# Top-k searches of a hidden expert selection placed behind each head's scores; exponential and step lengths of the open selections moved

## The chip, the core and the metric

The kernel runs on one core of a Trainium2 chip. The metric is the device time of one execution in microseconds (us). Engines are named as in the profile: PE (TensorE, matrix products; PEld its weight loads), DVE (VectorE), ACT (ScalarE), POOL (GpSimd), SP (SyncE, which issues the DMAs).

## The reference, cut

Two layers of a backbone: layer 0 mixes by short convolution and grouped-query attention, layer 1 by a bidirectional recurrence (RWKV-7). After each mixer stands the PEER feed-forward network, and the change is in how its experts are selected.

```
def peer_ffn(xn, w_q, sub_keys, u_tab, v_tab):      # T tokens in chunks of 128
        q = (xc @ w_q).reshape(n, 8, 2, 128)                        # 8 heads, two halves
        s = einsum('nhpd,hpkd->nhpk', q, sub_keys)                  # scores against 2 x 128 keys
        s1, i1 = top_k(s[:, :, 0], 16);  s2, i2 = top_k(s[:, :, 1], 16)
        cand_s = s1[..., :, None] + s2[..., None, :]                # 256 candidates of a head
        cand_i = i1[..., :, None] * 128 + i2[..., None, :]
        top_s, pos = top_k(cand_s, 16);  idx = take_along_axis(cand_i, pos)
        gate = softmax(top_s)
        act = gelu(einsum('nd,nhkd->nhk', xc, u_tab[idx]))
        return einsum('nhk,nhkd->nd', gate * act, v_tab[idx])
```

There are 128 x 128 = 16384 experts of width 1024, 256 latent and 256 context tokens. Layer 0 runs the network for both streams, layer 1 for the latent stream alone.

## The kernel before, in words

**Dense experts.** The kernel doesn't gather rows of the tables. It runs through all 16384 experts in 128 blocks E of 128, for 256 tokens at once (a pass); layer 0 has two passes, E = 0 to 255, layer 1 one. For each E: `prep_u` splits a block of the first table into a high part (uh, on ACT) and a low part (ul, half on DVE and half on POOL); `first` makes 24 products on PE (L1249 to L1251) and ACT's gelu (L1121); `gate` multiplies by the gate matrix G on DVE (L1128), splits the product into gwh (ACT) and gwl (DVE, both through `split`, L1244 and L1245); `second` makes 12 products with the second table (L1143), whose split `prep_v` leaves vl to POOL. G holds for each token the softmax weight of each expert, and is made by `gen` = `spread` (one-hots on DVE: oh L1029, eq L1033, two A L1035) and `gather` (32 products on PE, L1045, and a copy on ACT, L1046), 16 steps for 32 blocks of experts. A has one buffer.

**Selection.** The class `TopK` has three parts, all mainly on DVE. `keys` finds the 16 best of 128 scores, 4 columns a head (two halves, two blocks of 128 tokens), five instructions each (L83 to L87). `pair` takes two heads: candidates (L107), their best 16 (L117 to L121), the differences tm to the best (L125), the exponential of tm on ACT (L126), then the indices by comparisons and sums (L132 to L165, the helper `pick` among them), and the normalised weights (L170 to L175). It yields three times between these parts. `finish` transposes the results on PE.

**Open selection.** `Peer.start` runs twice, ahead of the first pass of layer 0 (about 300 to 506 us) and ahead of the pass of layer 1 (about 2900 to 3101 us). Tasks are written by generators: `score` and `keys` of eight heads, `ahead` (32 first products, W0 to W31, which need no selection), and `finish` (transposes, casts to i16 and g16, then 16 steps `gen`). `weave` takes the task with the lowest clock next and adds the number that it yields, so these numbers set the order in which the instructions are written; a list scheduler then places them on the engines.

**Hidden selection.** The selection of layer 0's second pass is done during its first: `select_shadow` is a generator that `beside` steps through in four slots of each E, from E = 32 to 92, such that NSEL = 162.4 units are spread evenly over them (2.7 for one E). A yield without a number is 1.0; WKEYS and WPAIR are 2.2. It makes the norm of the second chunk, then for each head two strips of the score weights (wh, wl), the products, and the score tile sc, which it stores to DRAM (sD). When all eight heads' scores are there, it opens the pool sht, loads the scores back (scl) and runs `keys` and `pair` over all heads one behind the other.

## Time and profile before

| | |
|---|---|
| median of 3 runs | 3780.04 us (3778.81 to 3786.54) |
| the profiled execution, its own time | 3783.13 us |
| its span in the profile | 3781.4 us |
| mean granted clock of PE | 0.943 |
| PE busy | 3411.8 us (90%) |
| DVE busy | 2511.7 us (66%) |
| ACT busy | 1728.7 us (46%) |
| POOL busy | 1754.1 us (46%) |

Busy time is the sum of an engine's instructions; the shares are means over stages with different limits, so they don't say which engine sets the pace in one stage. The profiled execution is one run of the program: its times are compared with each other, and its own time, not the median, is what a sum of its rows starts from. An idle time in brackets behind a row, or a wait, names what ended it.

### The profile page before, as it was taken

What the parts mean: (1) busy time and instruction counts of PE and PEld (TensorE: products, weight loads), DVE (VectorE), ACT (ScalarE), POOL (GpSimd) and SP (SyncE); (2) the same over time, 40 slices, a digit from 0 to 9 for tenths busy, and PEclk for the clock granted to TensorE, in tenths of its full rate; (3) what the DMA queues carried; (4) which work ended last, traced back from release to release, by engine and by line L of the source; (5) the groups of instructions that cost most, each with busy time, mean ns of one, the idle gap of its engine ahead of it and who ended that gap; (6) DMA issues with size and microseconds to landing.
All of it is one profiled execution on the core that took longest, in us unless ns stands there. A gap on an engine that the chain in (4) does not pass through costs nothing.

```text
span 3781.4 us, 74053 instructions
## 1 busy us (share of the span) xinstructions
PE 3411.8 (90%) x29543; PEld 2980.4 (79%) x29543; DVE 2511.7 (66%) x5230; ACT 1728.7 (46%) x2813; POOL 1754.1 (46%) x984
## 2 busy tenths in 40 slices
PE   7998789999889989999999999887787788999999
PEld 5678777998778778987788788786676776888898
DVE  3569887558964447546777655376878889666522
ACT  4343445554444445555444444453223345555544
POOL 1121644655455545444333333433434543666676
PEclk9999899999999999999999999987698889999999
DMA  7364655876588977775555565551024334555554
GB/s 237 122 217 151 218 174 194 265 249 226 191 293 287 323 256 240 248 236 191 193 180 191 182 218 192 189 167 37 21 68 139 112 102 150 179 179 179 178 186 155
DMA packets 337538, 710.57 MB, mean 188 GB/s; under 512 B 41220, under 2 KB 199560, under 8 KB 336168
## 3 DMA queue, kind: packets, MB, share of 16 engines
q1 hardware_dynamic: 337192, 705.84, 56.0%
q8 instruction: 231, 3.78, 0.4%
q14 instruction: 115, 0.94, 0.1%
HBM read 624.45 MB, written 81.30 MB: 187 GB/s over the span
## 4 chain that ended last, share of the span: by engine, by line
PE 56%; DVE 23%; issue 5%; POOL 3%; DMA 2%; ACT 2%; SPq 0%; DVEq 0%; POOLq 0%; ACTq 0%
PE acc L1143 19%; PE mm L1249 9%; PE mm L1250 9%; PE mm L1251 9%; DVE A L1035 3%; DVE mm L1128 2%; DVE oh L1029 2%; DVE prod L465 1%; PE mm L1045 1%; DVE TT L468 1%; DVE eq L1033 1%; PE mm L840 1%; PE mm L730 1%; DVE wl L1245 1%; DVE gwl L1245 1%
## 5 line engine op out<-in xcount | busy, mean ns | idle before, releaser
L1245 POOL TENSOR_TENSOR vl<-raw,vh 128x1024 fp32r<-128x1024 f32 x352 | 877.9, 2494 | 857.3 <-ACT vh L1244 773.8
L1249 PE MATMUL mm<-xh,uh 128*128 128x256 f32 x3072 | 909.6, 296 | 38.5 <-ACT uh L1097 35.1
L1250 PE MATMUL mm<-xh,ul 128*128 128x256 f32 x3072 | 898.0, 292 | 35.5 <-DVE ul L1102 22.9
L1251 PE MATMUL mm<-xl,uh 128*128 128x256 f32 x3072 | 889.2, 289 | 0.0
L1102 POOL TENSOR_TENSOR ul<-raw,uh 128x512 fp32r<-128x512 f32 x320 | 498.8, 1568 | 485.1 <-ACT uh L1097 441.5
L1249 PEld LDWEIGHTS mm<-xh,uh 128*128 128x128 f32 x3072 | 608.3, 198 | 57.3 <-ACT uh L1097 37.7
L1250 PEld LDWEIGHTS mm<-xh,ul 128*128 128x128 f32 x3072 | 610.1, 199 | 50.3 <-DVE ul L1102 27.2
L1251 PEld LDWEIGHTS mm<-xl,uh 128*128 128x128 f32 x3072 | 610.1, 199 | 16.1 <-issue 16.1
L1143 PE MATMUL acc<-vh,gwh 128*128 128x512 f32 x1536 | 499.9, 406 | 12.3 <-ACT gwh L1244 9.3
L1244 ACT CAST vh<-raw 128x1024 fp32r<-128x1024 f32 x384 | 403.1, 1050 | 232.4 <-issue 124.4
L1143 PE MATMUL acc<-vh,gwl 128*128 128x512 f32 x1536 | 484.4, 396 | 5.3 <-DVE gwl L1245 4.3
L1143 PE MATMUL acc<-vl,gwh 128*128 128x512 f32 x1536 | 482.9, 396 | 5.5 <-POOL vl L1245 5.4
L1128 DVE TENSOR_TENSOR mm<-mm,G 128x256 f32<-128x256 f32 x320 | 136.5, 427 | 470.3 <-ACT mm L1121 469.7
L1035 DVE TENSOR_TENSOR A<-eq,g 128x512 f16<-128x512 f16 x384 | 330.2, 886 | 115.5 <-PE mm L1045 64.7
L1097 ACT CAST uh<-raw 128x1024 fp32r<-128x1024 f32 x384 | 399.8, 1042 | 8.3 <-DMA raw<-in_peer_u_dram 8.1
L1121 ACT ACTIVATE mm<-mm 128x256 f32<-128x256 f32 x320 | 119.3, 373 | 512.4 <-PE mm L1251 509.0
L1143 PEld LDWEIGHTS acc<-vh,gwl 128*128 128x128 f32 x1536 | 289.0, 189 | 79.5 <-DVE gwl L1245 12.7
L1143 PEld LDWEIGHTS acc<-vl,gwh 128*128 128x128 f32 x1536 | 289.6, 190 | 74.7 <-POOL vl L1245 10.1
L1143 PEld LDWEIGHTS acc<-vh,gwh 128*128 128x128 f32 x1536 | 262.8, 191 | 57.9 <-ACT gwh L1244 12.0
L1029 DVE TENSOR_TENSOR oh<-iotaR,i 128x2048 f16<-128x2048 f16 x192 | 257.5, 1341 | 19.0 <-ACT i L939 16.7
L1244 ACT CAST gwh<-mm 128x256 fp32r<-128x256 f32 x384 | 142.9, 375 | 266.3 <-DVE mm L1128 263.4
L1102 DVE TENSOR_TENSOR ul<-raw,uh 128x512 fp32r<-128x512 f32 x192 | 187.1, 974 | 86.0 <-ACT uh L1097 85.9
(418 smaller groups left out, 5969.2 us busy)
## 6 DMA issues: line engine op xcount, KB each, us to landing
raw<-in_peer_u_dram SPq DMA_DIRECT2D x384, 512.0 KB
raw<-in_peer_v_dram SPq DMA_DIRECT2D x384, 512.0 KB
low<-ul SPq DMA_DIRECT2D x128, 512.0 KB
ul<-low SPq DMA_DIRECT2D x128, 512.0 KB
wraw<-in_ada_w_dram SPq DMA_DIRECT2D x48, 1024.0 KB
wraw<-in_peer_wq_dram SPq DMA_DIRECT2D x16, 1024.0 KB
wraw<-in_ev_w_in_dram SPq DMA_DIRECT2D x9, 1024.0 KB
wraw<-in_ev_w_out_dram SPq DMA_DIRECT2D x8, 1024.0 KB
```

Of the source, the lines that this page charges most:

```text
L1029: V.tensor_tensor(oh, self.iotaR[:, None].to_broadcast([128, 8, 128, 2]), per_token(i16[:, 1]).to_broadcast([128, 8, 128, 2]), ALU.is_equal)
L1035: V.tensor_tensor(A[:, i], eq, per_token(g16[:, i]).to_broadcast(sh), ALU.mult)
L1097: k.S.copy(uh, ur)
L1102: (le or (k.V, k.P)[i]).tensor_sub(ul[:, t], ur[:, t], uh[:, t].bitcast(F32))
L1121: self.k.S.activation(W, H, AF.Gelu)
L1128: self.k.V.tensor_mul(W2, W, self.GT[E // 32][:, E % 32])
L1143: self.k.T.matmul(self.ACC[n][2 * tb + dh], lhsT=a[:, 128 * tb:128 * tb + 128], rhs=b[:, 512 * dh:512 * dh + 512], start=e == 0 and a is w ...
L1244: self.last_copy = self.S.copy(hi, src).ins
L1245: (le or self.V).tensor_sub(lo, src, hi.bitcast(F32))
L1249: self.T.matmul(out, lhsT=ah, rhs=bh, start=start, stop=False)
L1250: self.T.matmul(out, lhsT=al, rhs=bh, start=False, stop=False)
L1251: self.T.matmul(out, lhsT=ah, rhs=bl, start=False, stop=stop)
```

## The change

Three edits. In `pair`, the exponential of tm is emitted behind the comparison g2 of its last part instead of in its first part. In `Peer.start`, a step of `keys` yields 2.9 instead of 1.1, and a step of `gen` 3.2 instead of 2.0. In `select_shadow`, the keys of a head follow directly behind its scores, and a pair directly behind its second head; scores are read from the tile sc, with no store to DRAM and no load back (16 of each fall away); the keys are loaded by heads, 128x256 eight times instead of 128x512 four times; and the pool sht is opened together with shw. The number of units of the hidden selection and its start and end stay.

```diff
@@ -123,7 +123,6 @@
         tm = tile([4, 16], F32, "tm")
         T4 = T16.rearrange("p b h k -> p (b h) k")
         V.tensor_tensor(tm, T4, T4[:, :, 0:1].to_broadcast([128, 4, 16]), ALU.subtract)
-        k.S.activation(tm, tm, AF.Exp)
         yield
 
         XF = tile([2, 16, 4], F16, "XF")
@@ -165,6 +164,7 @@
         V.tensor_sub(bb, PF, bb)
         g2 = tile([16, 16, 4], F16, "ge")
         V.tensor_tensor(g2, over_a(bb), over_k(k.io16), ALU.is_equal)
+        k.S.activation(tm, tm, AF.Exp)
         pick(g2, XF[:, 1], sel[:, 1])
         z = tile([2, 4], F32, "z")
         V.tensor_reduce(z[:, 0], tm, axis=AX.X, op=ALU.add)
@@ -906,7 +906,7 @@
         def keys(hd):
             for a in range(2):
                 tk.keys(hd, a, sc[hd][:, a])
-                yield 1.1
+                yield 2.9
             if hd % 2:
                 for _ in tk.pair(hd // 2):
                     yield 4.0
@@ -945,7 +945,7 @@
             yield 2.0
             for j in range(16):
                 self.gen(0, j)
-                yield 2.0
+                yield 3.2
 
         tasks = {}
         for hd in range(8):
@@ -1719,8 +1719,6 @@
     def select_shadow(self, layer, st, hd, xD, iD):
 
         I, tc, S, T, Y = self.I, self.tc, self.S, self.T, self.Y
-        sD = [self.dp.tile([128, 16, 128], F32, name=f"sD{i}") for i in range(2)]
-        kD = self.dp.tile([128, 16, 128], F32, name="kD")
         with tc.tile_pool(name="shx", bufs=1, reuse_waits="tile") as px:
             xs = [px.tile([128, 8, 256], F32R, name=f"xs{i}") for i in range(2)]
             with tc.tile_pool(name="shn", bufs=1, reuse_waits="tile") as pn:
@@ -1734,14 +1732,15 @@
                     self.split(xs[0][:, k], xs[1][:, k], xT[:, k], self.P)
                     yield
                 Y.dma_start(xD, xT)
-            with tc.tile_pool(name="shw", bufs=1, reuse_waits="tile") as pw:
+            with tc.tile_pool(name="sht", bufs=1, reuse_waits="tile") as pool, tc.tile_pool(name="shw", bufs=1, reuse_waits="tile") as pw:
+                tk = TopK(self, pool, f"{layer}s")
                 ws = self.strips(pw, self.score_specs(layer, 128), ahead=0, n=128, nr=1, nh=1)
                 for q in range(4):
-                    kT = pw.tile([128, 4, 128], F32, name="keysT")
-                    Y.dma_start(kT, I["peer_keys"][layer][:, 4 * q:4 * q + 4])
-                    yield
                     for hh in range(2):
                         hd_ = 2 * q + hh
+                        kT = pw.tile([128, 2, 128], F32, name="keysT")
+                        Y.dma_start(kT, I["peer_keys"][layer][:, 2 * hd_:2 * hd_ + 2])
+                        yield 0.5
                         qs = pw.tile([128, 2, 256], F32, name="qs")
                         for c in range(2):
                             wh, wl = next(ws)
@@ -1757,32 +1756,25 @@
                         pv = p.rearrange("p (a c k) -> p a c k", a=2, c=2)
                         for a in range(2):
                             for c in range(2):
-                                T.matmul(pv[:, a, c], lhsT=qs[:, c, 128 * a:128 * a + 128], rhs=kT[:, 2 * hh + c], start=True, stop=True)
+                                T.matmul(pv[:, a, c], lhsT=qs[:, c, 128 * a:128 * a + 128], rhs=kT[:, c], start=True, stop=True)
                         yield
                         sc = pw.tile([128, 2, 2, 128], F32, name="sc")
                         S.copy(sc, pv)
-                        for a in range(2):
-                            Y.dma_start(sD[a][:, 2 * hd_:2 * hd_ + 2], sc[:, a])
                         yield
-        with tc.tile_pool(name="sht", bufs=1, reuse_waits="tile") as pool:
-            tk = TopK(self, pool, f"{layer}s")
-            for hd_ in range(8):
-                for b in range(2):
-                    sc = pool.tile([128, 2, 128], F32, name="scl", bufs=3)
-                    Y.dma_start(sc, sD[b][:, 2 * hd_:2 * hd_ + 2])
-                    tk.keys(hd_, b, sc)
-                    yield WKEYS
-                if hd_ % 2:
-                    for _ in tk.pair(hd_ // 2):
+                        for b in range(2):
+                            tk.keys(hd_, b, sc[:, b])
+                            yield WKEYS
+                    for _ in tk.pair(q):
                         yield WPAIR
                     yield WPAIR
-            def put(b, p):
-                iT = pool.tile([128, 3, 128], F32, name="iT", bufs=2)
-                S.copy(iT, p)
-                Y.dma_start(iD[:, :, 128 * b:128 * b + 128], iT)
-
-            tk.finish(put, self.mm)
-            yield
+
+                def put(b, p):
+                    iT = pool.tile([128, 3, 128], F32, name="iT", bufs=2)
+                    S.copy(iT, p)
+                    Y.dma_start(iD[:, :, 128 * b:128 * b + 128], iT)
+
+                tk.finish(put, self.mm)
+                yield
 
 
     def rwkv_cols(self):
```

Where this moves instructions, in the order in which each engine has them:

In the hidden selection, DVE before the change. gate mm, ul and gwl are the ordinary work of an expert, A, oh and eq the one-hots; the first search is the row L83, and all others follow from there on:

```order
L1128 TENSOR_TENSOR mm_9970<-mm_9970,G_6823 128x256
L1102 TENSOR_TENSOR ul_10083<-raw_9960,uh_10081 128x512
L1245 TENSOR_TENSOR gwl_10078<-mm_9970,gwh_10077 128x256
L1035 TENSOR_TENSOR A_10179<-eq_10180,g16_4206 128x512 x2
L1029 TENSOR_TENSOR oh_10362<-iotaR_3276,i16_4205 128x2048
L1033 TENSOR_TENSOR eq_10365<-iotaR_3276,i16_4205 128x512
L1128 TENSOR_TENSOR mm_10088<-mm_10088,G_6823 128x256
L1102 TENSOR_TENSOR ul_10172<-raw_10086,uh_10170 128x512
L1245 TENSOR_TENSOR gwl_10167<-mm_10088,gwh_10166 128x256
L83 MAX M_10148<-scl_10151 128x8 x2
L84 MAX_INDEX X_10149<-M_10148,scl_10151 128x8
```

DVE after the change, at its first search. wl is the low part of score weights, which before stood ahead of every search:

```order
L1245 TENSOR_TENSOR gwl_7928<-mm_7815,gwh_7927 128x256
L1245 TENSOR_TENSOR wl_8552<-wraw_7832,wh_8551 128x1024
L1035 TENSOR_TENSOR A_8006<-eq_8007,g16_4566 128x512 x2
L1029 TENSOR_TENSOR oh_8200<-iotaR_3216,i16_4565 128x2048
L1033 TENSOR_TENSOR eq_8203<-iotaR_3216,i16_4565 128x512
L1128 TENSOR_TENSOR mm_7938<-mm_7938,G_5415 128x256
L1102 TENSOR_TENSOR ul_7999<-raw_7936,uh_7997 128x512
L83 MAX M_7129<-sc_7990 128x8
L1245 TENSOR_TENSOR gwl_7994<-mm_7938,gwh_7993 128x256
L84 MAX_INDEX X_7130<-M_7129,sc_7990 128x8
L85 MATCH_REPLACE s2_8024<-M_7129,sc_7990 128x128
L83 MAX M_7129<-sc_7990 128x8
```

The first search now follows on its head's scores, with the weights of later heads still to come; it is the first of eight such bursts of keys, every second with a pair behind it, and between them lie the scores of the next head.

In the open selection of layer 1, ACT before the change, at its fourth exponential (tm; W is the gelu of a first product, uh the cast for one):

```order
L1121 ACTIVATE W8_34638<-mm_34613 128x256
L1097 CAST uh_34697<-raw_34640 128x1024
L126 ACT_TABLE_LOAD
L126 ACTIVATE tm_34922<-tm_34922 128x64
L1121 ACT_TABLE_LOAD
L1121 ACTIVATE W9_34693<-mm_34668 128x256
L1097 CAST uh_34767<-raw_34695 128x1024
```

ACT after the change, at the same place:

```order
L1121 ACTIVATE W8_34511<-mm_34486 128x256
L1097 CAST uh_34573<-raw_34513 128x1024
L167 ACT_TABLE_LOAD
L167 ACTIVATE tm_35185<-tm_35185 128x64
L1121 ACT_TABLE_LOAD
L1121 ACTIVATE W9_34557<-mm_34532 128x256
L1097 CAST uh_34622<-raw_34559 128x1024
```

The exponential stands between the same W8 and W9 (its line number is that of the instruction ahead of its new place); the other seven of the open selections stay between their gelus in the same way.

Further on in the same stage, ACT before the change, where the indices (i16, g16) are cast and the copies G of the gathers begin:

```order
L1097 CAST uh_35114<-raw_35041 128x1024
L1121 ACTIVATE W17_35094<-mm_35069 128x256
L939 CAST i16_35098<-acc_35100 128x2x128
L940 ACTIVATE g16_35099<-acc_35100 128x128
L939 CAST i16_35098<-acc_35107 128x2x128
L940 ACTIVATE g16_35099<-acc_35107 128x128
L1097 CAST uh_35190<-raw_35096 128x1024
L1121 ACTIVATE W18_35144<-mm_35119 128x256
L1097 CAST uh_35306<-raw_35146 128x1024
L1046 COPY G_35148<-acc_35156 128x16x32
L1121 ACTIVATE W19_35220<-mm_35195 128x256
```

ACT after the change, at the same casts:

```order
L1121 ACTIVATE W27_35391<-mm_35366 128x256
L939 CAST i16_35395<-acc_35397 128x2x128
L940 ACTIVATE g16_35396<-acc_35397 128x128
L939 CAST i16_35395<-acc_35404 128x2x128
L940 ACTIVATE g16_35396<-acc_35404 128x128
L1097 CAST uh_35487<-raw_35393 128x1024
L1121 ACTIVATE W28_35483<-mm_35458 128x256
L1097 CAST uh_35562<-raw_35485 128x1024
L1046 COPY G_35411<-acc_35419 128x16x32
L1121 ACTIVATE W29_35517<-mm_35492 128x256
L1097 CAST uh_35637<-raw_35519 128x1024
L1046 COPY G_35411<-acc_35528 128x16x32
```

The casts moved from behind W17 to behind W27. Before, copies G and gelus alternate from there to W31; after, four copies stand among the last four gelus, and twelve follow with no gelu between them, behind two casts vh and two casts uh for the first experts of the loop. In layer 0 the casts stay where they were, and five gathers instead of about one for each gelu stand ahead of W31, eleven behind it.

## Rows read from the trace of the kernel before

**Rows 1.** The page's chain that ended last, by engine.

```profile
PE 56%; DVE 23%; issue 5%; POOL 3%; DMA 2%; ACT 2%; SPq 0%; DVEq 0%; POOLq 0%; ACTq 0%
```

**Rows 2.** Windows: length, busy PE, PEld, DVE, ACT, POOL, PE clock, DMA share, GB/s.

```profile
694.50:881.00 186.50, 186.50 (x1593) 172.04 (x1592) 99.33 (x125) 95.55 (x139) 112.81 (x54) 1.00 0.75 245
881.00:898.80 17.80, 17.80 (x142) 16.08 (x140) 16.24 (x76) 8.94 (x14) 11.40 (x6) 1.00 0.85 293
898.80:1087.00 188.20, 163.63 (x1266) 144.24 (x1264) 184.16 (x612) 85.37 (x123) 94.40 (x49) 0.94 0.61 207
```

**Rows 3.** Timeline of ACT (start, duration): gelus two experts apart.

```profile
886.67 0.37 ACT L1121 ACTIVATE mm<-mm 128x256 f32<-128x256 f32 x1 [2.29 <-PE mm L1251]
...
898.77 0.37 ACT L1121 ACTIVATE mm<-mm 128x256 f32<-128x256 f32 x1 [2.23 <-PE mm L1251]
```

**Rows 4.** DVE by line, 694.5 to 881 us: count, busy us, mean ns.

```profile
L1035 DVE TENSOR_TENSOR A<-eq,g 128x512 f16<-128x512 f16 x24 | 35.3, 1508 | 14.0 <-PE mm L1045 14.0
...
L1245 DVE TENSOR_TENSOR wl<-wraw,wh 128x1024 fp32r<-128x1024 f32 x6 | 7.3, 1222 | 9.0 <-ACT wh L1244 9.0
```

**Rows 5.** DVE by line, 898.8 to 1087 us.

```profile
L1035 DVE TENSOR_TENSOR A<-eq,g 128x512 f16<-128x512 f16 x24 | 22.7, 979 | 0.0
```

**Rows 6.** Waits, 898.8 to 1087 us: total us, times, longest us.

```profile
ACT gwh L1244 <- DVE mm L1128: 89.9, 22, 7.8
...
ACT tm L126 <- DVE tm L125: 10.4, 4, 3.9
```

**Rows 7.** Timeline of DVE at the first searches of the hidden selection.

```profile
881.44 0.42 DVE L1128 TENSOR_TENSOR mm<-mm,G 128x256 f32<-128x256 f32 x1
...
884.44 0.49 DVE L83 MAX8 M<-scl 128x8 f32<-128x128 f32 x2 [1.09 <-DMA scl<-sD]
...
920.80 0.41 DVE L1128 TENSOR_TENSOR mm<-mm,G 128x256 f32<-128x256 f32 x1
```

**Rows 8.** A window of 5 us in the same place.

```profile
920.00:925.00 5.00, 3.44 (x26) 3.05 (x25) 5.00 (x16) 3.56 (x5) 2.36 (x1) 1.00 0.44 143
```

**Rows 9.** Timeline of DVE, open selection of layer 1: two key columns.

```profile
2981.02 0.28 DVE L83 MAX8 M<-sc 128x8 f32<-128x128 f32 x1
...
2982.19 0.28 DVE L83 MAX8 M<-sc 128x8 f32<-128x128 f32 x1
```

**Rows 10.** Timeline of ACT, open selection of layer 0: gelus.

```profile
389.85 0.38 ACT L1121 ACTIVATE W<-mm 128x256 f32<-128x256 f32 x1 [1.87 <-PE mm L1251]
...
393.00 0.38 ACT L1121 ACTIVATE W<-mm 128x256 f32<-128x256 f32 x1 [1.83 <-PE mm L1251]
...
430.81 0.38 ACT L1121 ACTIVATE W<-mm 128x256 f32<-128x256 f32 x1 [2.84 <-PE mm L1251]
```

**Rows 11.** Timeline of DVE, gathers of layer 0.

```profile
441.81 2.89 DVE L1035 TENSOR_TENSOR A<-eq,g 128x512 f16<-128x512 f16 x2
...
445.78 0.76 DVE L1035 TENSOR_TENSOR A<-eq,g 128x512 f16<-128x512 f16 x2 [0.62 <-PE acc L1045]
446.45 1.22 DVE L1029 TENSOR_TENSOR oh<-iotaR,i 128x2048 f16<-128x2048 f16 x1
447.59 0.42 DVE L1033 TENSOR_TENSOR eq<-iotaR,i 128x512 f16<-128x512 f16 x1
...
499.55 1.66 DVE L1035 TENSOR_TENSOR A<-eq,g 128x512 f16<-128x512 f16 x2
```

**Rows 12.** Timeline of ACT, open selection of layer 1.

```profile
2988.79 0.26 ACT L126 ACTIVATE tm<-tm 128x64 f32<-128x64 f32 x1 [12.51 <-DVE tm L125]
...
3012.79 0.38 ACT L1121 ACTIVATE W<-mm 128x256 f32<-128x256 f32 x1 [1.55 <-PE mm L1251]
...
3015.72 0.38 ACT L1121 ACTIVATE W<-mm 128x256 f32<-128x256 f32 x1 [1.61 <-PE mm L1251]
```

**Rows 13.** Timeline of DVE, layer 1: first one-hot, last A.

```profile
3016.45 1.34 DVE L1029 TENSOR_TENSOR oh<-iotaR,i 128x2048 f16<-128x2048 f16 x1 [11.24 <-ACT i L939]
...
3093.16 1.67 DVE L1035 TENSOR_TENSOR A<-eq,g 128x512 f16<-128x512 f16 x2
```

## The prediction

> **What bounds the kernel now.** I read the chain of waits first, then busy time by windows, then single rows on VectorE (DVE) and ScalarE (ACT). By engine the chain is TensorE (PE) 56% and DVE 23% [rows 1]: most of the run is a PE-bound expert loop, and the change can only pay where DVE sets the pace. Three stretches of the first pass show where that is [rows 2]. From 694.5 to 881 us (24 experts, with the second chunk's norm and scores in the shadow) PE is busy 186.50 of 186.50 us and DVE 99.33. From 898.8 to 1087 us (again 24 experts, the searches in the shadow) PE is busy 163.63 of 188.20 and DVE 184.16: this stretch is DVE's, and one expert takes 188.2/24 = 7.84 us. When PE is full, two experts take 898.77 - 886.67 = 12.10 us, 6.05 each [rows 3]. So the second stretch is 188.2 - 24 x 6.05 = **43.0 us** longer than PE needs, and nothing done to these searches can give more than that. How DVE holds PE there is in the waits: ACT waited 89.9 us for DVE's gate product before it could make gwh [rows 6].
>
> **Searches in the shadow.** The same searches are done before and after; what changes is where they stand. Before, all of them follow the last score. After, they come in bursts between the scores of E = 32 to 92. Nothing is saved on DVE, but the slack of the first stretch (99.33 of 186.5) is used.
> DVE's ordinary work per expert is (99.33 - 7.3)/24 = 3.83 us, the 7.3 being score weights [rows 2, 4]. The searches then took 184.16 - 24 x 3.83 = 92.2 us in the second stretch and 16.24 - 3 x 3.83 = 4.8 us in the 17.8 us ahead of it [rows 2]: 97 us, 24.2 for a pair of heads. One column of keys costs 2982.19 - 2981.02 = 1.17 us (open selection of layer 1, the same instructions) [rows 9]; a pair of heads has eight columns, 9.4 us, so `pair` is 24.2 - 9.4 = 14.8 us.
> The whole shadow has 162.4 units for 60 experts, 2.7 each. Even heads: four key columns (4.7 us) stand inside about 1.6 experts; with 1.6 x 3.83 = 6.1 us that is 10.8 us against 9.7 us of PE, and the 1.1 us lag goes away in the following five experts of scores, where DVE needs 3.83 of 6.05. Odd heads: keys 4.7 + pair 14.8 = 19.5 us stand within about 4.5 experts, whose own work is 17.2: 36.7 us on DVE against 4.5 x 6.05 = 27.2 on PE, a lag of **9.5 us**. How much lag does PE bear? Before, the searches begin at 884.44 [rows 7]; the gates at 881.44 and 920.80 are five expert intervals apart (four gates lie between), 39.4 us where PE needs 5 x 6.05 = 30.25, so DVE is 9.1 us late, and just there PE drops to 3.44 of 5 us [rows 7, 8]. So 9.5 of lag meets a tolerance of about 9.1. The bare difference is 0.4 us; I take 2 us a pair, since the tolerance was read at a point where PE had begun to lose. Four pairs: 8 us. Gain 43 - 8 = **35 us** (ends: 43 with no stall, 9 in rival B). What is late next is PE itself, at 6.05 us per expert.
> The stores of scores to DRAM and their loads fall away. The one wait on them that DVE shows is 1.09 us [rows 7]; it was hidden behind a full PE. The keys come in eight loads instead of four, with the same bytes, and SP's queue loses 32 issues: zero, at most 1 us either way. Holding the score tile until its keys are read can't delay the next head's copy, which stands some six experts later. In the shadow the exponential moves behind DVE's last part; ACT waited 10.4 us for its input, four times [rows 6]. That wait goes, but ACT is then held by the gates anyway, so it is inside the 43.
>
> **Exponential in the open selections.** I cost it at zero. In layer 1 ACT stood 12.51 us before the fourth exponential, until 2988.79 [rows 12]. That would be worth having, but in the order ACT's eight rows of it stand between the same gelus as before: emitted later, scheduled to the same place. See rival D.
>
> **Open gathers, layer 1.** Before, indices are ready behind W17, DVE starts its one-hots at 3016.45, and 16 gathers alternate with 14 first products; the last A begins at 3093.16 and lasts 1.67 [rows 13]: (3093.16 - 3016.45)/16 = 4.8 us a gather. After, the index transposes stand ten first products later. These run at 3015.72 - 3012.79 = 2.93 us [rows 12], so the one-hots start near 3015.7 + 29.3 = 3045. Four gathers lie among the last four first products (4 x 4.8 = 19.2, to 3064), then twelve come bare. A bare one needs on DVE A 0.76 + one-hot 1.22 + eq 0.42 = 2.40 us, and on PE less: after the A that began at 441.81 and took 2.89, the next A could begin at 445.78, 1.08 us later, once its buffer had been read [rows 11]. 12 x 2.40 = 28.8, to 3093 against 3094.8: -2, and with the first experts' value splits already made by ACT in between, **-3** (ends -8, +6).
>
> **Open gathers, layer 0.** Up to W18 at 430.81 [rows 10] ACT's order is unchanged. Then 13 first products, 3.15 us each (393.00 - 389.85) [rows 10], carry only five gathers instead of about one each: 41 us, to 472, and eleven bare gathers take 11 x 2.40 = 26.4, to 498. Before, the last A ended at 499.55 + 1.66 = 501.2 [rows 11]. **-2** after something for the five gathers beside the products (ends -6, +6).
>
> **Sum.** -35 - 3 - 2 = -40 on the profiled run: 3783.13 - 40 = 3743. That run (span 3781.4) lies 3.1 us above the median of the runs shown, 3780.04, so on the scale of the median **3740 us**.
>
> **Rival B: the bursts stay DVE's.** DVE's A took 1508 ns on average in the first stretch, where GpSimd (POOL) was busy 112.81 of 186.5 us (60%), and 979 ns in the second, where it was busy 94.40 of 188.2 (50%) [rows 2, 4, 5]: the same instruction costs 1.54 times as much beside a busier POOL. If all of `pair` were stretched like that when it stands beside the first kind of work, 14.8 x 0.54 = 8.0 us more a pair, the lag is 17.5, the stall 8.4, and four of them 34 us: the shadow gains only 9, and the time is 3780 - 9 - 5 = 3766. Against it: the 24.2 us a pair were themselves measured beside a POOL that was half busy, and in a stall POOL runs dry too, which frees DVE.
> The Trainium skill says the same of the cause ("SBUF — State Buffer", section "Who interferes with whom"): a VectorE operation with two SBUF inputs contends with a GpSimd operation that reads SBUF, and the pair of ports is an exclusive lock. The trace agrees for A, by its two means; taken to its end for every instruction of `pair`, the rule gives this rival's 3766, and without it the forecast's 3740.
>
> **Rival C, slower: bare gathers don't run bare.** If POOL's reads (low parts and value splits of the next experts) lie beside all bare gathers, A costs 2.89 as at 441.81 [rows 11], and a gather 2.89 + 1.22 + 0.42 = 4.53 us. 23 bare gathers x 2.13 = +49, against the -40: 3789. It decides against the change from 2.40 + 40/23 = 4.1 us a gather. For it: the 4.8 us of now. Against: in layer 1 only two value splits and two key casts stand among the twelve in ACT's order, so POOL has work for a part of them; and the 4.8 holds a first product of 2.93.
>
> **Rival D: the exponential does leave ACT's way** (DVE's rows run otherwise than the order says). Then the 12.51 us before the fourth exponential are freed for gelus and casts of the first products: up to 12.5 more, 3728.
>
> **How the numbers follow.** Forecast (bursts nearly absorbed, gathers near even) 0.62; B 0.2; C 0.06; D 0.05; the rest, 0.07, for gains that come back as a wait I don't see, around zero. The likeliest is 3740. Range: the low end is the whole 43 with both gathers near their better ends (-43 - 8 - 6 = -57, less a little that can't all happen): 3724. The high end is B with the gathers at +6 in one layer: 3766 + 6 = 3772. C and most of the rest are left out above, D mostly inside. 0.2% is 7.6 us, about what a measurement of this kernel can tell from no change. Forecast, D and nearly all of B are faster by more: 0.84. Within: 0.09, a little of B and half the rest. Slower: 0.07.
>
> **What would show it.** In the profile after, the 51 experts from the one whose gelu is at 694.5 to the one at 1087.0 should take about 392.5 - 35 = 358 us, with PE over 97% busy and DVE some 75 to 80% throughout; ACT's wait for the gate should fall from 89.9 us to under 40, in four clusters at the odd heads' bursts. B would show as A, one-hot and `pair` rows of 1.3 us and more there, with PE idle in each burst. In the open selections ACT should still wait over 10 us for an exponential's input (D if not), DVE should idle some 40 us in layer 1 before its first one-hot, and then bare gathers should follow each other at 2.4 us (C if over 4). The forecast is wrong if PE loses more than 5 us a pair, or if the stages up to the first gates of either layer are over 8 us longer.

## The result, and the profile after

The changed kernel takes 3741.87 us (median of 5 runs, 3738.35 to 3744.55); the kernel before took 3782.74 us beside it (5 runs, 3778.81 to 3786.54). The ratio is 0.9895, with a 95% interval of 0.9883 to 0.9906: 1.05%, or 40 us, faster. The profiled run of after has a span of 3741.8 us, against 3781.4 before.

The gain lies almost whole in the first pass. Two gelus (ACT, column 1 the start in us) bound it: that of expert block E = 32, the first with the shadow beside it, and that of E = 112, 20 blocks behind the end of the hidden selection. One row each, before:

```profile
617.77 0.36 ACT L1121 ACTIVATE mm<-mm 128x256 f32<-128x256 f32 x1
```

```profile
1246.79 0.37 ACT L1121 ACTIVATE mm<-mm 128x256 f32<-128x256 f32 x1 [0.77 <-PE mm L1251]
```

After:

```profile
617.54 0.36 ACT L1121 ACTIVATE mm<-mm 128x256 f32<-128x256 f32 x1
```

```profile
1211.77 0.37 ACT L1121 ACTIVATE mm<-mm 128x256 f32<-128x256 f32 x1 [0.83 <-PE mm L1251]
```

1246.79 - 617.77 = 629.0 us before, 1211.77 - 617.54 = 594.2 us after: **34.8 us** less. E = 32 itself comes at the same time in both, so the open selection of layer 0 gave nothing. From E = 112 to 255 after is 7.0 us shorter (1175.4 against 1182.4), but the kernel with the step lengths alone, which is no faster in all, reads 1176.3 there, so I don't count that as gain. The same gelus give the length of every stretch in every kernel that was profiled, and show how good one profile of a stretch is: after and the five kernels that differ from it in the hidden part alone have the same code in the first column, and read 258.9 to 265.5. From E = 32 to 112 the three kernels with the searches where they stood before read 628.7 to 634.2, and the five with the changed kernel's searches at its weights (after, hidden part alone, and the three with one exponential that keep them whole) 594.2 to 602.9: in the mean 33 us less.

| profiled kernel | layer 0, E 0 to 32 | E 32 to 92 (searches) | E 92 to 112 | layer 0's last block to layer 1's first | layer 1, E 0 to 32 |
|---|---|---|---|---|---|
| before | 265.9 | 469.2 | 159.8 | 517.3 | 266.4 |
| after | 264.9 | 449.0 | 145.2 | 520.6 | 265.7 |
| hidden part alone | 266.6 | 448.8 | 146.3 | 520.6 | 266.9 |
| step lengths alone | 262.4 | 471.8 | 162.4 | 518.3 | 266.7 |
| exponential alone | 267.4 | 468.8 | 159.9 | 522.0 | 266.5 |
| after, scores through DRAM | 260.0 | 469.2 | 148.0 | 516.7 | 267.3 |
| after, wider bursts | 259.3 | 455.1 | 145.9 | 524.2 | 268.0 |
| after, narrower bursts | 258.9 | 461.1 | 147.4 | 520.6 | 265.4 |
| after, no searches | 265.5 | 431.5 | 147.7 | 520.6 | 264.2 |
| after, one exponential | 278.6 | 450.4 | 147.7 | 507.7 | 258.8 |
| the same, transposes held | 260.0 | 455.2 | 147.8 | 508.5 | 257.8 |
| the same, steps of 1.7 and 2.7 | 256.7 | 450.8 | 147.7 | 506.4 | 261.3 |
| after, pieces of half the size | 260.8 | 444.3 | 144.7 | 515.2 | 267.8 |
| pieces of half the size, one exponential, held, steps of 1.7 and 2.7 | 257.0 | 452.7 | 147.7 | 506.4 | 261.3 |

Windows of the profile after answer to those of [rows 2] (length; busy PE, PEld, DVE, ACT, POOL, each with its instructions; granted clock; DMA share; GB/s). The first runs from the gelu of E = 41 to that of E = 65, the third from E = 68 to E = 92, the fourth to E = 112:

```profile
689.85:868.83 178.98, 171.97 (x1441) 156.82 (x1440) 146.77 (x367) 92.21 (x131) 102.41 (x52) 0.98 0.69 230
868.83:890.45 21.62, 21.62 (x174) 19.88 (x173) 19.18 (x49) 10.85 (x16) 14.34 (x7) 1.00 0.76 259
890.45:1066.57 176.12, 171.12 (x1431) 154.90 (x1430) 150.83 (x366) 89.96 (x131) 106.46 (x52) 0.99 0.72 242
1066.57:1211.77 145.20, 144.51 (x1316) 117.65 (x1315) 79.69 (x114) 69.75 (x109) 80.62 (x40) 1.00 0.94 330
```

DVE is now busy 146.77 of 178.98 and 150.83 of 176.12 us, where it had 99.33 and then 184.16 [rows 2]: the same work is spread. PE's share in the third window rises from 87 to 97%. From E = 32 to 112, before and then after (columns as above):

```profile
617.77:1246.79 629.02, 587.37 (x4920) 516.64 (x4921) 419.56 (x982) 299.21 (x440) 348.76 (x171) 0.97 0.75 252
617.54:1211.77 594.23, 575.45 (x4906) 508.75 (x4907) 445.22 (x982) 301.38 (x442) 348.76 (x171) 0.98 0.76 260
```

PE idles 41.7 us before and 18.8 after: 22.9 of the 34.8. The other 11.9 are PE's own busy time, for nearly the same products at a granted clock of 0.97 and 0.98. DVE has 982 instructions in both, and they take 25.7 us more after.

What PE itself waits for in the 51 experts from E = 41 to 92 (total us, times, longest) is almost only the low part `ul` of the first table, which DVE makes for the next first product. Before, and then after:

```profile
PE mm L1250 <- DVE ul L1102: 22.3, 13, 3.0
PE mm L1250 <- DVE ul L1102: 10.1, 4, 5.0
```

The four waits of after end at 740.74, 842.40, 956.72 and 1051.58 us, one for each pair of heads (5.04, 1.85, 1.33 and 1.91 us). ACT's wait for the gate, which the prediction read as the way in which DVE holds PE [rows 6], did not fall in the same 51 experts:

```profile
ACT gwh L1244 <- DVE mm L1128: 92.6, 29, 7.8
ACT gwh L1244 <- DVE mm L1128: 103.2, 39, 5.8
```

In the third window alone it is 53.9 us where it was 89.9, but the first window now has 43.2 where it had 2.7. PE lost less while ACT waited more, so this wait is no measure of PE's loss.

**What lies behind E = 92.** Of the 34.8 us only 20.2 are there at E = 92; 14.6 come in the next 20 blocks, which before took 159.8 us. Windows of before in that stretch:

```profile
1087.00:1095.00 8.00, 4.54 (x60) 3.96 (x58) 7.04 (x8) 5.27 (x9) 7.47 (x4) 1.00 1.04 343
1095.00:1105.00 10.00, 8.58 (x66) 6.40 (x66) 0.56 (x3) 1.79 (x3) 2.38 (x1) 0.83 1.07 366
1125.00:1130.00 5.00, 0.56 (x3) 0.14 (x1) 5.00 (x5) 0.00 (x0) 1.94 (x1) 1.00 0.96 297
```

and PE's waits of before from 1087 to 1137 us:

```profile
PE mm L1359 <- DMA wraw<-in_ada_w_dram: 4.9, 1, 4.9
PE mm L1045 <- DVE A L1035: 4.7, 1, 4.7
```

PE is busy 148.77 of the 159.79 us from E = 92 to 112 before, and 144.51 of 145.20 after. Two waits make 9.6 of the 11.0 us of before: PE stands for the next shadow's weights (L1359, strips of 1 MB, with the DMA engines at a share above 1.0 in the first two rows), and at 1125 us for DVE, which makes the second pass's indices and one-hots only then. The SP queue shows why these were late together: before, the finish of the hidden selection was followed by two strips at once, and by the load of the indices 23 us later,

```profile
1086.77 1.34 SPq L1782 DMA_DIRECT2D iD<-iT  x2
...
1089.30 1.11 SPq L1255 DMA_DIRECT2D wraw<-in_ada_w_dram  x2
...
1109.60 0.80 SPq L968 DMA_DIRECT2D it<-iD  x1
```

and after, the strips come one by one and the indices are loaded 16 us behind their store:

```profile
1066.34 1.34 SPq L1774 DMA_DIRECT2D iD<-iT  x2
...
1073.11 0.39 SPq L1255 DMA_DIRECT2D wraw<-in_ada_w_dram  x1
...
1079.13 0.38 SPq L1255 DMA_DIRECT2D wraw<-in_ada_w_dram  x1
...
1082.18 0.42 SPq L968 DMA_DIRECT2D it<-iD  x1
```

Every kernel whose searches stand among the scores takes 145 to 148 us here, whatever its bursts and with or without the round trip through DRAM, and so does the one without searches; every kernel that has them behind the scores takes 160 to 162. So this part hangs on where the searches stand. That the two strips and the late indices are the cause is read from these rows and was not tried by itself.

**The open selections.** ACT still waits for the exponential's input (L126 before, L167 after). Before, in layer 0 and in layer 1:

```profile
ACT tm L126 <- DVE tm L125: 21.5, 4, 7.9
```

```profile
ACT tm L126 <- DVE tm L125: 31.0, 4, 12.5
```

After:

```profile
ACT tm L167 <- DVE tm L125: 22.8, 4, 7.8
```

```profile
ACT tm L167 <- DVE tm L125: 25.1, 4, 10.8
```

The bare gathers of layer 1, DVE after the change (start, duration, idle time before it and what ended it):

```profile
3003.51 1.37 DVE L1029 TENSOR_TENSOR oh<-iotaR,i 128x2048 f16<-128x2048 f16 x1 [42.79 <-ACT i L939]
...
3021.12 3.85 DVE L1035 TENSOR_TENSOR A<-eq,g 128x512 f16<-128x512 f16 x2
...
3026.97 2.28 DVE L1245 TENSOR_TENSOR vl<-raw,vh 128x1024 fp32r<-128x1024 f32 x1
...
3047.49 0.76 DVE L1035 TENSOR_TENSOR A<-eq,g 128x512 f16<-128x512 f16 x2 [0.62 <-PE acc L1045]
...
3050.78 0.75 DVE L1035 TENSOR_TENSOR A<-eq,g 128x512 f16<-128x512 f16 x2
...
3052.61 0.76 DVE L1035 TENSOR_TENSOR A<-eq,g 128x512 f16<-128x512 f16 x2 [0.62 <-PE acc L1045]
...
3061.01 0.75 DVE L1035 TENSOR_TENSOR A<-eq,g 128x512 f16<-128x512 f16 x2
...
3062.14 0.76 DVE L1128 TENSOR_TENSOR mm<-W,G 128x256 f32<-128x256 f32 x2
```

DVE idles 42.79 us ahead of its first one-hot. The bare stretch begins when the fourth A ends, at 3024.97, with one value split (vl) and two low parts (ul, 0.68 us each) still in it. Later two gathers take 3052.61 - 3047.49 = 5.12 us, 2.56 each. The last A begins at 3061.01, the first gate at 3062.14. Before, the last A ended at 3094.8 [rows 13], but the first gate came at 3101.47, since other work (casts and splits of the first experts) lay in between:

```profile
3101.47 1.83 DVE L1128 TENSOR_TENSOR mm<-W,G 128x256 f32<-128x256 f32 x2
```

3101.47 - 3062.14 = 39.3 us, against 38.7 at the stage's first gelu (2946.47 before, 2907.81 after): up to its first gate the stage is shorter by 0.6 us, although its last A ends 5.6 us later, counted from that gelu (3061.76 - 2907.81 against 3094.83 - 2946.47). In layer 0 the last A and the first gate of after are at

```profile
509.30 0.76 DVE L1035 TENSOR_TENSOR A<-eq,g 128x512 f16<-128x512 f16 x2 [0.62 <-PE acc L1045]
510.38 0.77 DVE L1128 TENSOR_TENSOR mm<-W,G 128x256 f32<-128x256 f32 x2 [0.31 <-ACT G L1046]
```

so the last A ends 9 us later than before (510.1 against 501.2 [rows 11]), the first gate comes 3.8 us later than before's, which began at 506.63, and the first block behind the 32 prepared ones at the same time (617.54 against 617.77).

### The profile page after: what moved, and what is told of

Same layout as the page of the kernel before. It is cut to its first block, busy times and chain, and to the rows that moved or that the text cites. A ratio compares the mean times of both kernels' runs of the same rounds, so it can differ in the third digit from the quotient of the medians.

```text
span 3741.8 us, 73990 instructions
## 1 busy us (share of the span) xinstructions
PE 3392.8 (91%) x29543; PEld 2965.4 (79%) x29543; DVE 2490.3 (67%) x5230; ACT 1730.8 (46%) x2813; POOL 1747.7 (47%) x984
## 5 line engine op out<-in xcount | busy, mean ns | idle before, releaser
L1245 POOL TENSOR_TENSOR vl<-raw,vh 128x1024 fp32r<-128x1024 f32 x352 | 878.4, 2495 | 902.1 <-ACT vh L1244 822.9
L1249 PE MATMUL mm<-xh,uh 128*128 128x256 f32 x3072 | 900.2, 293 | 32.5 <-ACT uh L1097 28.5
L1250 PE MATMUL mm<-xh,ul 128*128 128x256 f32 x3072 | 886.7, 289 | 25.4 <-DVE ul L1102 10.7
L1251 PE MATMUL mm<-xl,uh 128*128 128x256 f32 x3072 | 879.9, 286 | 0.0
L1102 POOL TENSOR_TENSOR ul<-raw,uh 128x512 fp32r<-128x512 f32 x320 | 490.9, 1544 | 417.5 <-ACT uh L1097 401.1
L1249 PEld LDWEIGHTS mm<-xh,uh 128*128 128x128 f32 x3072 | 599.4, 195 | 50.9 <-ACT uh L1097 30.1
L1250 PEld LDWEIGHTS mm<-xh,ul 128*128 128x128 f32 x3072 | 600.5, 195 | 38.6 <-POOL ul L1102 14.0
L1251 PEld LDWEIGHTS mm<-xl,uh 128*128 128x128 f32 x3072 | 600.6, 196 | 2.9 <-issue 2.9
L1128 DVE TENSOR_TENSOR mm<-mm,G 128x256 f32<-128x256 f32 x320 | 136.6, 427 | 429.6 <-ACT mm L1121 428.7
L1035 DVE TENSOR_TENSOR A<-eq,g 128x512 f16<-128x512 f16 x384 | 307.1, 826 | 124.1 <-PE mm L1045 59.1
L1143 PEld LDWEIGHTS acc<-vh,gwl 128*128 128x128 f32 x1536 | 289.4, 189 | 77.5 <-DVE gwl L1245 11.3
L1143 PEld LDWEIGHTS acc<-vh,gwh 128*128 128x128 f32 x1536 | 262.5, 191 | 53.9 <-ACT gwh L1244 8.2
L1029 DVE TENSOR_TENSOR oh<-iotaR,i 128x2048 f16<-128x2048 f16 x192 | 257.8, 1343 | 45.7 <-ACT i L939 45.4
```

The lines of the kernel that those rows point to most:

```text
L1029: V.tensor_tensor(oh, self.iotaR[:, None].to_broadcast([128, 8, 128, 2]), per_token(i16[:, 1]).to_broadcast([128, 8, 128, 2]), ALU.is_equal)
L1035: V.tensor_tensor(A[:, i], eq, per_token(g16[:, i]).to_broadcast(sh), ALU.mult)
L1102: (le or (k.V, k.P)[i]).tensor_sub(ul[:, t], ur[:, t], uh[:, t].bitcast(F32))
L1128: self.k.V.tensor_mul(W2, W, self.GT[E // 32][:, E % 32])
L1143: self.k.T.matmul(self.ACC[n][2 * tb + dh], lhsT=a[:, 128 * tb:128 * tb + 128], rhs=b[:, 512 * dh:512 * dh + 512], start=e == 0 and a is w ...
L1245: (le or self.V).tensor_sub(lo, src, hi.bitcast(F32))
```

## Experiments

The theory under test: the whole gain is that DVE's slack among the scores is used; the two edits in the open selections are worth nothing. The rivals: that the step lengths carry a part; that ACT was set free by the exponential; that what counts is the round trip through DRAM that fell away.

### One edit at a time

The hidden selection's part alone (in the changed kernel, the two other edits taken back):

```diff
+        k.S.activation(tm, tm, AF.Exp)
         yield
...
-        k.S.activation(tm, tm, AF.Exp)
...
-                yield 2.9
+                yield 1.1
...
-                yield 3.2
+                yield 2.0
```

> The hidden selection's part alone: keys behind each head's scores, no round trip through DRAM; the open selections and the place of the exponential as before. Theory (the whole gain is DVE's slack among the scores being used, the other two edits are worth nothing): 3742 to 3748 us, that is 35 to 41 us under the kernel before. Rival (the open selections' step lengths carry a part, since the experts after the shadow also came earlier): over 3752 us.

Measured: 3745.4 us, ratio to the kernel before 0.9894 (0.9879 to 0.9908), the same as the full change, and as the theory had it. From E = 32 to 112 it took 595.1 us, the full change 594.2.

The step lengths alone (1.1 to 2.9 and 2.0 to 3.2 in the kernel before):

> The step lengths of the open selections alone (2.9 and 3.2), all else as before. Theory: within 3 us of the kernel before, though the last gather of layer 0 ends 9 us later and the first expert behind the 32 prepared ones comes at the same time. My prediction had put -5 on it. Rival: 8 us or more faster.

Measured: 3781.11 us, ratio 0.9999 (0.9990 to 1.0008), as the theory had it.

The exponential alone:

```diff
-        k.S.activation(tm, tm, AF.Exp)
...
         V.tensor_tensor(g2, over_a(bb), over_k(k.io16), ALU.is_equal)
+        k.S.activation(tm, tm, AF.Exp)
```

> The exponential's place alone. Theory: within 3 us of the kernel before in time; ACT still waits 20 us and more for the exponential's input in each open selection. Rival (ACT set free): 10 us or more faster, with that wait under 10 us.

Measured: 3785.87 us, ratio 1.0000 (0.9990 to 1.0010); ACT still waited 21.6 us in layer 0 and 30.3 in layer 1 for the exponential's input, as the theory had it. So one edit of three carries the gain. The step lengths move many instructions and no time; the exponential moves in the text and not on ACT.

### Position or round trip

In the changed kernel (the tiles sD in DRAM are declared as before):

```diff
                         S.copy(sc, pv)
+                        for a in range(2):
+                            Y.dma_start(sD[a][:, 2 * hd_:2 * hd_ + 2], sc[:, a])
                         yield
                         for b in range(2):
+                            Y.dma_start(sc[:, b], sD[b][:, 2 * hd_:2 * hd_ + 2])
                             tk.keys(hd_, b, sc[:, b])
```

> The changed kernel, but each head's scores are stored to DRAM and loaded back into the same tile ahead of its keys. Theory (position is what counts): within 4 us of the changed kernel, 3740 to 3748. Rival (DVE's waits for the scores from DRAM were what cost): most of the gain gone, over 3760.

Measured: 3767.67 us, ratio 0.9961 (0.9949 to 0.9973). Most of the gain is gone, 25 us of 40, and the time is over 3760: the rival's numbers held, the theory's did not. Position alone leaves 15 us, and by the table none of it lies among the searches: E = 32 to 92 takes 469.2 us as before the change, and what is gained stands behind E = 92 (148.0 against 159.8). DVE's wait for the scores in this run, from 600 to 1090 us,

```profile
DVE M L83 <- DMA sc<-sD: 29.4, 10, 5.8
```

and in the changed kernel:

```profile
DVE M L83 <- ACT sc L1762: 6.0, 4, 3.1
```

What PE waits for in the round trip's run, E = 41 to 92:

```profile
PE mm L1250 <- DVE ul L1102: 18.5, 9, 4.1
PE mm L183 <- DVE sel L156: 7.5, 1, 7.5
```

The rival's reason holds only in the new place. When the scores were long stored, the round trip cost one wait of 1.09 us [rows 7]; right behind the scores it costs 29.4, and everything that is queued on DVE behind the first search, the low parts for PE included, waits too. So the position needs the scores in the tile, if the search stands directly behind them. A round trip with the search placed one head later, so that the load has time to land, was not tried. The prediction's "zero" for the round trip was right for the place where it stood, and said nothing of the new place.

### What the spread searches still cost

This kernel leaves the searches out, and the second pass gets indices of zero:

```diff
+                self.V.memset(tk.sel, 0.0)
...
                         for b in range(2):
-                            tk.keys(hd_, b, sc[:, b])
                             yield WKEYS
-                    for _ in tk.pair(q):
+                    for _ in range(3):
                         yield WPAIR
```

> The changed kernel without the searches of the hidden selection (keys and pair are left out, the selected indices of the second pass are zeros); scores and their placement stay. It measures what the searches still cost. Theory: PE is busy all through experts 40 to 92, and the time falls by 5 to 15 us, to 3727 to 3737. Rival (the spread searches still hold PE up as the burst did): falls by over 20 us.

Measured: 3723.24 us, ratio 0.9835 (0.9819 to 0.9852). The 51 experts from E = 41 to 92 (same columns as above):

```profile
694.25:1050.79 356.54, 356.54 (x3036) 325.84 (x3035) 215.13 (x261) 186.23 (x265) 220.91 (x109) 1.00 0.75 252
```

PE is busy all through, as the theory had it, but the time fell by 23 us by the ratios (0.9895 against 0.9835), so the size was the rival's. From E = 32 to 112 this run took 579.2 us. So the searches cost 629.0 - 579.2 = 49.8 us there before, and 594.2 - 579.2 = 15.0 after; by the five kernels with the same searches it is 15.0 to 23.7, which the ratios' 23 fit. In the 51 experts after takes 376.72 us, 20.2 more: 12.0 are PE idle (10.1 of them the four waits for `ul`), and 8.2 are PE's busy time, 364.71 against 356.54 us at granted clocks of 0.99 and 1.00.

### The width of a burst

Narrower bursts (and further down wider ones), by the weights alone:

```diff
-WKEYS, WPAIR, WPROJ = 2.2, 2.2, 1.7
+WKEYS, WPAIR, WPROJ = 1.5, 1.0, 1.7
```

> The changed kernel with the weights of the hidden searches lowered to 1.5 (keys) and 1.0 (a step of pair): bursts stand in about 3.2 experts each, and DVE's lag at their end rises from 9.5 to about 12.4 us. Theory of lag against tolerance: 3 us more stall in each of four bursts, 3752 to 3757 us. Rival (the order of searches and scores is all that counts, not the width of a burst): within 3 us of the changed kernel.

Measured: 3753.76 us, ratio 0.9919 (0.9903 to 0.9935), 9 us slower than the changed kernel by the ratios, within the theory's range. The 51 experts take 386.9 us, 10.2 more than after's 376.7. But PE's waits there are not what the theory says:

```profile
PE mm L1250 <- DVE ul L1102: 12.0, 3, 5.0
PE mm L183 <- DVE sel L156: 8.9, 1, 8.9
```

At the first three pairs PE waits 5.04, 3.48 and 3.48 us for `ul`, 3.8 more than the 8.2 of the changed kernel's first three, where 3 more for each were expected. The largest single wait, 8.9 us, stands at the end of the selection: the index transposes (L183) have been placed on PE ahead of its next products, and wait there for the last pair. So the time came out as forecast, and some of it by the lag, but most by a wait that the theory did not have.

```diff
-WKEYS, WPAIR, WPROJ = 2.2, 2.2, 1.7
+WKEYS, WPAIR, WPROJ = 3.5, 5.0, 1.7
```

> The changed kernel with the weights of the hidden searches raised from 2.2 and 2.2 to 3.5 (keys) and 5.0 (a step of pair), so that a pair's burst is spread over about 7 experts instead of 4.5. Theory of lag against tolerance: DVE's lag at the end of a burst falls from 9.5 to about 4 us, under what PE bears, and the 8 us that I charged for four bursts come back: 3733 to 3739 us. Rival (PE's rest idle time in the shadow has other causes, such as waits for the scores): within 3 us of the changed kernel.

Measured: 3747.01 us, ratio 0.9895 (0.9879 to 0.9912), no difference to the changed kernel, as the rival had it; 601.0 us from E = 32 to 112. The expected 8 us did not come, and the stall itself did not shrink: from E = 41 to 92 PE waits 12.7 us in 7 waits for `ul` (the longest 5.3), where the changed kernel waits 10.1 in 4. That stretch is 6.3 us shorter (370.4), but the units are shared by all steps, so more score products are pressed into E = 32 to 41, which takes 84.7 us instead of 72.3 (606 instructions of PE against 552).

Pieces of half the size at the same places (in `keys` a yield behind each column pair, eight in `pair` instead of four, at 1.1):

```diff
-                            tk.keys(hd_, b, sc[:, b])
-                            yield WKEYS
-                    for _ in tk.pair(q):
-                        yield WPAIR
-                    yield WPAIR
+                            for _ in tk.key_steps(hd_, b, sc[:, b]):
+                                yield WKEYS / 2
+                    for _ in tk.pair(q, True):
+                        yield WPAIR / 2
+                    yield WPAIR / 2
```

> The changed kernel with the same weights and places of the hidden searches, but cut into pieces of half the size (a yield of 1.1 behind each pair of key columns and eight in a pair instead of four). Theory (the remaining loss, 16 us by the run without searches, is gates and low parts waiting behind a piece of searches of 3 to 4 us on DVE): half of it comes back, 3731 to 3738 us. Rival (DVE's whole lag over a burst is what counts): within 3 us of the changed kernel.

Measured: 3740.21 us, ratio 0.9889 (0.9874 to 0.9904). No difference that these runs resolve, as the rival had it; PE's wait for `ul` is 11.3 us in 5. So over all these widths and pieces the wait stays between 10.1 and 12.7 us: the sign of the lag is seen only in the narrow bursts, and why a pair costs PE what it does was not found by these runs.

### Setting ACT free in the open selections

Rival D of the prediction could not happen by the change, since the exponential kept its place; here it is brought about. The differences tm of all four pairs are kept in sel, and one exponential and one normalisation stand in `finish`, held behind the last gelu that was written ahead of it. The class is shared, so the hidden selection gets the same edit:

```diff
...
+        with k.tc.issue_after(k.last_gelu):
+            k.S.activation(self.sel[:, :, 2], self.sel[:, :, 2], AF.Exp)
+        for b in range(2):
+            V.tensor_reduce(z[:, b], ex[b], axis=AX.X, op=ALU.add)
+        V.reciprocal(z, z)
+        for b in range(2):
+            V.tensor_tensor(ex[b], ex[b], z[:, b, :, :, None].to_broadcast([128, 4, 2, 16]), ALU.mult)
```

> The changed kernel with one exponential and normalisation for all four pairs of a selection, in its finish, held behind the last gelu that was written ahead of it. ACT no longer waits for DVE's tm (22.8 us in layer 0, 25.1 in layer 1 of the changed kernel). Theory (those waits hold up the first products, as rival D of the prediction assumed): the two stages get shorter by 10 to 20 us each, 3702 to 3722 us. Rival (the gathers behind them or the stage of second products end at the same time anyway): within 8 us of the changed kernel.

Measured: 3738.55 us, ratio 0.9877 (0.9861 to 0.9893), 7 us better than the change by the ratios, which is the rival's size for a reason that neither had. ACT's waits for tm are gone: the stretch from layer 0's last block through layer 1's first 32 takes 507.7 + 258.8 = 766.5 us, 19.8 less than after the change. But in layer 0 another wait has taken their place. One row of ACT and PE's wait of this run, layer 0:

```profile
423.99 0.38 ACT L1121 ACTIVATE W<-mm 128x256 f32<-128x256 f32 x1 [23.44 <-PE mm L1251]
```

```profile
PE acc L183 <- DVE sel L155: 18.6, 2, 14.1
```

ACT now idles 23.44 us for PE, and PE stands in front of the index transposes (L183): those of the indices no longer wait for the exponential, and had been placed ahead of first products that were ready. Layer 0's E 0 to 32 grew from 264.9 to 278.6 us, and ate most of it.

With the transposes held too, at the changed kernel's step lengths (made after the next one):

```diff
+                with k.tc.issue_after(k.last_mm):
+                    k.T.transpose(p[:, 128 * i:128 * i + 128], self.sel[:, b, i], k.ident)
```

> The run with one exponential and held transposes, but with the step lengths of the changed kernel (2.9 and 3.2), so that exponential and transposes stand behind W27 and twelve gathers come bare. It tells the waits taken away from the place of the gathers. Theory (the waits are what was gained): 3718 to 3728 us, near the run with 1.7 and 2.7 at 3719.86. Rival (the earlier gathers carry the gain, the waits only moved): 3734 to 3742.

Measured: 3722.25 us, ratio 0.9833 (0.9817 to 0.9849), as the theory had it. And with steps of 1.7 and 2.7, so that the gathers come seven first products earlier:

> As the run with one exponential, and the index transposes on PE are held behind the last first product that was written ahead of them, and a step of keys in the open selections yields 1.7 and one of gen 2.7, so that exponential, transposes and gathers stand behind W20. In layer 0 of that run PE stood 14 us in front of the transposes (they had been placed ahead of products that were ready), and the first expert behind the prepared ones came 13 us later than before. Theory (ACT's and then PE's wait for the selection is what the stage loses, and it can be taken away): the first gates of both layers come 10 to 20 us earlier than in the changed kernel, 3705 to 3722 us. Rival (the stage of second products behind it is bound by DVE's next gathers and gives it back): within 8 us of the changed kernel.

Measured: 3719.86 us, ratio 0.9837 (0.9823 to 0.9850). The two are equal, so the waits were the gain (some 22 us over the change), and the place of the gathers is worth nothing here too. Of the held kernel at 2.9 and 3.2, the stretch from layer 0's last block through layer 1's first 32 takes 508.5 + 257.8 = 766.3 us, after the change 520.6 + 265.7 = 786.3: 20 us are in layer 1, where some exponentials stand ahead of the stage's first gelu, and where the single exponential alone had given as much. What holding the transposes added is layer 0's first column, 260.0 us instead of 278.6. The edit also takes two table loads of 1.28 us out of each open selection, 2.6 us, which is too little to be the 20. The hidden selection did not gain by it: E = 32 to 112 takes 602.9 us, after 594.2. This is the version that beats both kernels. With the finer pieces of the hidden searches:

> Both of these together. They lie in different stages, so their differences to the changed kernel should add up within 4 us.

Measured: 3718.67 us, ratio 0.9828 (0.9815 to 0.9842); the two add up within 4 us as expected, and the pieces add nothing that can be told from the last.

## Why the prediction was right, and where not

Forecast were 3740 us and -40; measured are 3741.87 and, against the runs beside it, -40.9. Step by step:

- **The hidden searches, -35.** Measured from E = 32 to 112: -34.8. The cause named, that DVE's slack among the scores is used, fits the part up to E = 92, where PE's waits for DVE fell by half. But the sum of -35 is right by luck: its two terms are not, nor is its place. Up to E = 92, where the forecast looked, the gain is 20.2 us (469.2 to 449.0), and in the 51 experts named it is 15.8: they were to take 358 us and took 376.7. The ceiling of 43.0 was too high there: without searches E = 32 to 92 takes 431.5, 37.7 less than before. The stall of 8 us was too small: 449.0 - 431.5 = 17.5 are left. The missing 14.6 us came behind E = 92, where the rows of before show PE's waits for strips and indices, and where the prediction had put nothing.
- **How DVE holds PE.** Not by the gate, as I read from ACT's 89.9 us: PE's own waits are for `ul`, 22.3 us before and 10.1 after, while ACT's wait for the gate rose from 92.6 to 103.2. It was the wrong row to read, and its mark (under 40) failed. PE was to be over 97% busy and is 96 to 100% by window; DVE was to be 75 to 80% busy and is 82 to 89%.
- **Lag against tolerance.** The four stalls at the four pairs came as drawn, and PE's own wait, 10.1 us, is near the 8 charged. What is late besides is PE's busy time, 8.2 us more than without searches, which the prediction did not have. That the stall follows the lag was borne out in part for narrower bursts (3.8 us of the 9 expected at three pairs) and not for wider ones.
- **Round trip, zero.** Right in its old place; in the new one it would have cost some 25 us by the ratios (0.9961 against 0.9895). I had not priced it there, although the change would have lost most of its worth without that edit.
- **Exponential, zero.** Right, and for the reason given: ACT's wait was 21.5 and 31.0 us before, 22.8 and 25.1 after, and the exponential alone changed no time. The order told what the diff did not.
- **Open gathers, -3 and -2.** Both too good. Measured -0.6 to the first gate in layer 1, nothing at E = 32 in layer 0, and a ratio of 0.9999 for the step lengths alone. The last A came 5.6 us later in layer 1 and 9 us later in layer 0, where 2 earlier was forecast for each. In layer 1 the bare stretch from 3024.97 to the end of the last A at 3061.76 takes 36.8 us instead of 28.8: a bare gather takes 2.56 us instead of 2.40, since DVE's A waits 0.62 us at every second one for the buffer; the last A, which is the one I compared, is the thirteenth of the stretch and not the twelfth; and 3.6 us of splits for the first experts stand in it. That layer 1's gate came no later all the same is another thing that I had not priced: before, 6.6 us of other work lay between the last A and the gate, and after almost none.
- **Rival B** (bursts stay DVE's, 3766) didn't come. From E = 32 to 112 DVE is busy 445.22 us after and 336.51 without the searches:

```profile
619.26:1198.45 579.19, 570.21 (x4906) 505.77 (x4907) 336.51 (x431) 294.99 (x428) 345.81 (x171) 0.99 0.78 267
```

  So the searches cost DVE 108.7 us, 27.2 a pair, against the forecast's 24.2 and B's 32.2. What did get dearer than before is the ordinary work beside them: `eq` (L1033) took 456 ns on average before and 709 after. A took 1104 ns in the changed kernel, between the 1508 and 979 of [rows 4, 5], with POOL busy 57 and 60% in the two long windows, so POOL's share alone doesn't set it. DVE by line, 690 to 1066 us of after:

```profile
L1035 DVE TENSOR_TENSOR A<-eq,g 128x512 f16<-128x512 f16 x50 | 53.6, 1104 | 4.9 <-PE mm L1045 4.7
```

  The rule of the Trainium skill beside this rival ("SBUF — State Buffer", section "Who interferes with whom") is about VectorE operations with both inputs in SBUF, and fits where the rows grew dearer: both inputs of `eq` lie there, while the gate (L1128) and `gwl` (L1245), with one input from PSUM, stayed at 425 and 424 and at 416 and 413 ns, and the searches' MAX8 (L86) at 275 and 277. As the price of a whole burst the runs do not bear it out.

- **Rival C** didn't come, at 2.56 us a gather against its 4.1. **Rival D** didn't happen by this change; its mechanism is real, and worth about 22 us when ACT's waits and PE's wait for the transposes are both taken away.

## What to carry to other kernels

Work that is hidden beside a PE-bound loop belongs where its engine has slack, even if the number of its instructions stays; a whole stage's busy share doesn't show this, two windows side by side do. To see what the bound engine loses, read its own waits: here ACT's rose while PE's fell by half. Before a later position is worth anything, ask what its input waits for there: scores through memory cost almost nothing when old and most of the gain when fresh. An instruction that waits for a slow one holds up what is queued behind it on its engine (PE stood 14.1 us in front of the index transposes, with ready products behind them); it should be written, and held, behind the work that is ready; take one such wait away and look at once for the next instruction that has been placed ahead in its stead.

## What the runs showed of the hardware

While the bare gathers run alone, PE is granted its lower clock. After, 480 to 510 us in layer 0, and further on (columns as above):

```profile
480.00:510.00 30.00, 12.40 (x322) 10.33 (x323) 27.24 (x48) 11.37 (x12) 3.06 (x2) 0.51 0.35 119
530.00:560.00 30.00, 29.60 (x239) 23.02 (x238) 30.00 (x41) 16.11 (x23) 12.82 (x5) 1.00 0.50 160
```

PE is busy 12.40 of 30 us and the granted clock is 0.51, the 1.2 GHz level, where the gathers of the same stage before had first products between them and the clock was 0.92:

```profile
423.00:506.00 83.00, 65.82 (x906) 63.78 (x905) 68.58 (x73) 39.04 (x52) 45.16 (x30) 0.92 0.60 207
```

It cost little here, as I read the rows: a pair of bare gathers in layer 1 is filled by DVE's instructions but for a wait of 0.62 us, and from 530 us on the clock is at 1.00. What a higher clock would have given there was not tried.
